# A conv-FFN whose down-projection trails the up-projection: half of its columns as seven block products

## The chip, the cores and the metric

One core of a Trainium2 chip runs the whole layer. The metric is device time of one execution in microseconds (us). TensorE (PE) multiplies, its weight loads are listed as PEld, VectorE is DVE, ScalarE is ACT, GpSimd is POOL, and SyncE (SP) issues the DMA transfers from HBM to the on-chip memory SBUF. Matmuls accumulate in PSUM, which has eight banks of 128 x 512 f32.

## The reference, cut to what matters

The layer is an attention mixer and then a conv-FFN, each added to `x` (256 tokens, 2048 columns). The change concerns the FFN:

```
def conv_ffn(h, w_up_l, conv_w_l, conv_b_l, w_down_l):
    u = h @ w_up_l                                  # 256 x 2048 @ 2048 x 11264
    u = causal depthwise convolution of width 3 over the tokens, + conv_b_l
    gate, val = jnp.split(u, 2, axis=-1)            # 5632 each
    return (jax.nn.silu(gate) * val) @ w_down_l     # 256 x 5632 @ 5632 x 2048
...
h = rms_norm(x, ffn_norm[layer])
x = x + conv_ffn(h, w_up[layer], conv_w[layer], conv_b[layer], w_down[layer])
```

All is f32. The kernel gets near f32 out of one-pass matmuls by splitting each operand into a rounded part `hi` (type fp32r) and the rest `lo`, and adding three products: hi x hi, hi x lo, lo x hi.

## The kernel before

**Weights.** `weights` (L202) makes one tile of weights ready: a DMA of up to 1 MB into `w_raw` (three buffers, L209), an ACT cast to `w_hi` (L210) and a DVE subtraction to `w_lo` (L211), two buffers each. The pool `wpool` is opened at the start and stays open to the end. The three instructions get a higher priority by `AHEAD`; a scheduler orders each engine's instructions by priority and by which buffers are free, and puts in the waits. Each engine then works strictly in that order.

**Attention.** Until about 413 us: the input projection, two kinds of attention as generators that advance one `step` per weight tile, and the output projection. That last one is `token_major` (L220) with `x` updated at L556; beside it `transposed_split` (L147) makes `hT`, the transposed and split activations of the FFN.

**FFN.** 44 tiles of 128 features for gate and 44 for value. `up_pair` (L603) makes two feature tiles: `feature_major` (L242) runs 16 blocks of k in two halves, one weight tile each; per k it does two matmuls of `w_hi` against hi and lo of `hT` together (512 columns, L250) and two of `w_lo` against hi alone (256 columns, L255). The accumulator has two banks. `summed` (L262) adds its halves out of PSUM (ACT copy L265, DVE L266), L588 scales by the token's norm, `convolved` (L582) does the convolution (ACT L592, four DVE steps L597), and L620 to L624 make SiLU, the product with the value and the split pair `g2`. Accumulators rotate over three places: two of pool `psa` and one of `psf`.

**Order of work.** `FFN_PARTS` cuts the 44 tiles into parts of 16, 16 and 12. For each part all up pairs come first, then the down-projection of the part, by `token_major` in four chunks of 512 columns: per weight tile of four k tiles 24 matmuls (L235, L236, L237: two token tiles, three products), and one addition to `x` (L630) at the end of a chunk. The last part's chunks are stored (L633). The parameters of the convolution (`crow`) are loaded early, at L118.

Of the kernel before, what the change touches and what calls it, by code (L numbers as in the profile page):

```python
# [8 lines left out]
F32 = mybir.dt.float32  # L9
F32R = mybir.dt.float32r  # L10
AF = mybir.ActivationFunctionType
ALU = mybir.AluOpType
AX = mybir.AxisListType

P = 128
D = 2048
S = 256
NT = S // P
# [6 lines left out]
NFT = DFF // P  # L25
# [11 lines left out]

AHEAD = 200
WINDOW = 2
FFN_PARTS = [(0, 16), (16, 32), (32, 44)]  # L40


@with_exitstack
def hybrid_layer(
# [19 lines left out]
    nc = tc.nc  # L64
    act, dve = nc.scalar, nc.vector
# [3 lines left out]
    of = out.rearrange("b s d -> (b s) d")  # L69
    wi, wo, wu, wd = w_in[0], w_out[0], w_up[0], w_down[0]  # L70

    const = ctx.enter_context(tc.tile_pool(name="const", bufs=1))
    wpool = ctx.enter_context(tc.tile_pool(name="wpool", bufs=3))
    big = ctx.enter_context(tc.tile_pool(name="big", bufs=1))
    small = ctx.enter_context(tc.tile_pool(name="small", bufs=4))
    psa = ctx.enter_context(tc.tile_pool(name="psa", bufs=2, space=bass.MemoryType.PSUM))
    psb = ctx.enter_context(tc.tile_pool(name="psb", bufs=2, space=bass.MemoryType.PSUM))

    def f32(t):
        return t.bitcast(F32)  # L80


    NC2 = 2 * NFT
    cs = const.tile([P, C_MF], F32, name="cs")
    prow = const.tile([50, P], F32, name="prow")
    crow = const.tile([NC2, 4, P], F32, name="crow")
    bf = const.tile([P, NH], F32, name="bf")
    x2 = big.tile([P, NT, D], F32, name="x2")
    xt = [x2[:, t, :] for t in range(NT)]
# [18 lines left out]
    def load_parameters(masks):  # L108
        r0 = KT
        for src, n in (  # L110
            (ffn_norm, KT), (out_norm_fox, NH), (out_norm_sb, NH), (q_norm, 1), (k_norm, 1)
        ):
            nc.sync.dma_start(prow[r0 : r0 + n, :], src[0].rearrange("(n p) -> n p", p=P))
            r0 += n
        nc.sync.dma_start(cs[:, P:], cst[:, P:C_MF])
        nc.sync.dma_start(masks, cst[:, C_MF:])
        nc.sync.dma_start(bf, b_forget.to_broadcast([P, NH]))
        nc.sync.dma_start(crow[:, :3, :], conv_w[0].rearrange("w (n p) -> n w p", p=P))  # L118
        nc.sync.dma_start(crow[:, 3, :], conv_b[0].rearrange("(n p) -> n p", p=P))

    def rsqrt(out_, ss, scale, n):
        a = small.tile([P, n], F32, name="rs_a", tag=f"rs_a{n}")
# [55 lines left out]
            dve.tensor_scalar(dg[t], ident, rstd[:, t : t + 1], None, op0=ALU.mult)  # L178
        return rstd, dg

    def in_every_partition(dg, n):
        R = const.tile([P, S], F32, name=f"R{n}")
        pr = psb.tile([P, S], F32, name="pr", tag="t")
        for t in range(NT):
            nc.tensor.matmul(pr[:, t * P : (t + 1) * P], ones, dg[t], start=t == 0, stop=t == NT - 1)
        dve.tensor_copy(R, pr)
        return R


    waiting = deque()  # L190

    def step():
        for g in list(waiting)[:WINDOW]:
            if next(g, g) is g:
                waiting.remove(g)
# [3 lines left out]
            step()  # L199


    def weights(src, a, b):  # L202
        raw = wpool.tile([P, 2048], F32, name="w_raw", tag="w_raw")
        hi = wpool.tile([P, 2048], F32R, name="w_hi", tag="w_hi", bufs=2)
        lo = wpool.tile([P, 2048], F32R, name="w_lo", tag="w_lo", bufs=2)
        n = a * b
        r3 = raw[:, :n].rearrange("p (a b) -> p a b", a=a)
        with tc.high_priority(offset=AHEAD):
            nc.sync.dma_start(r3, src)  # L209
            act.copy(hi[:, :n], raw[:, :n])  # L210
            dve.tensor_tensor(lo[:, :n], raw[:, :n], f32(hi[:, :n]), op=ALU.subtract)  # L211
        return (
            hi[:, :n].rearrange("p (a b) -> p a b", a=a),
            lo[:, :n].rearrange("p (a b) -> p a b", a=a),
        )

    def rows_of(w, k0, n, c0, cols):
        return w[k0 * P : (k0 + n) * P, c0 : c0 + cols].rearrange("(k p) c -> p k c", p=P)
# [23 lines left out]
    def feature_major(w, c0, pool, tag):  # L242

        acc = pool.tile([P, 2, 512], F32, name="pu", tag=tag)
        for kh in range(2):
            hi, lo = weights(rows_of(w, 8 * kh, 8, c0, 2 * P), 8, 2 * P)
            for i in range(8):
                k = 8 * kh + i
                for j in range(2):
                    nc.tensor.matmul(  # L250
                        acc[:, j, :], hi[:, i, j * P : (j + 1) * P],
                        hT[:, k].rearrange("p a b -> p (a b)"), start=k == 0, stop=False,
                    )
                for j in range(2):
                    nc.tensor.matmul(  # L255
                        acc[:, j, S:], lo[:, i, j * P : (j + 1) * P], hT[:, k, 0, :],
                        start=False, stop=k == KT - 1,
                    )
            step()
        return acc  # L260

    def summed(pool, acc, tag, **kw):  # L262

        t2 = pool.tile([P, 2, S], F32, name="t2", tag=tag, **kw)
        act.copy(t2, acc[:, :, S:])  # L265
        dve.tensor_tensor(t2, acc[:, :, :S], t2, op=ALU.add)  # L266
        return t2

    with ExitStack() as actx:
        at = actx.enter_context(tc.tile_pool(name="at", bufs=1))  # L270
        pss = actx.enter_context(tc.tile_pool(name="pss", bufs=2, space=bass.MemoryType.PSUM))
        tmp = actx.enter_context(tc.tile_pool(name="tmp", bufs=2))
# [77 lines left out]
        rstd1, dg1 = token_factors(ss1, 1)  # L350
# [19 lines left out]
        for j in range(3):  # L370
            acc = project(2 * WF + 344 * j, 344)
# [97 lines left out]


        B0 = 3 * WF + NH
        R1 = in_every_partition(dg1, 1)
        R1q = const.tile([P, S], F32, name="R1q")
        dve.tensor_scalar(R1q, R1, QSCALE, None, op0=ALU.mult)

        def sb_heads(c0, scale, name):
# [87 lines left out]
    ccol = const.tile([P, 4, NC2], F32, name="ccol")  # L564
    R = None

    def convolution_parameters():
        for i in range(4):
            pc = psb.tile([P, 512], F32, name="pcc", tag="t")
            nc.tensor.transpose(pc[:, :NC2], crow[:, i, :], ident[:NC2, :NC2])  # L570
            dve.tensor_copy(ccol[:, i, :], pc[:, :NC2])


    ff = ctx.enter_context(tc.tile_pool(name="ff", bufs=2))
    psf = ctx.enter_context(tc.tile_pool(name="psf", bufs=1, space=bass.MemoryType.PSUM))
    nu = 4
    up = [ff.tile([P, 2, 2 + S], F32, name=f"up{i}") for i in range(nu)]
    for u in up:
        dve.memset(u[:, :, 0:2], 0.0)
    n_up = 0  # L580

    def convolved(ps, f0):  # L582

        nonlocal n_up
        u = up[n_up % nu]
        n_up += 1
        t2 = summed(ff, ps, "t2")
        dve.tensor_tensor(u[:, :, 2:], t2, R.unsqueeze(1).to_broadcast([P, 2, S]), op=ALU.mult)  # L588
        a = ff.tile([P, 2, S], F32, name="cv", tag="cv", bufs=4)
        for j in range(2):  # L590
            f = f0 + j
            act.activation(  # L592
                a[:, j, :], u[:, j, 2:], AF.Identity,
                scale=ccol[:, 2, f : f + 1], bias=ccol[:, 3, f : f + 1],
            )
            for w in range(2):
                dve.scalar_tensor_tensor(  # L597
                    a[:, j, :], u[:, j, w : w + S], ccol[:, w, f : f + 1], a[:, j, :],
                    op0=ALU.mult, op1=ALU.add,
                )  # L600
        return a

    def up_pair(f0):  # L603

        nonlocal R, n_pair
        pool, tag = (psf, "pu") if n_pair % 3 == 2 else (psa, "acc")
        n_pair += 1
        acc = feature_major(wu, f0 * P, pool, tag)
        if R is None:
            R = in_every_partition(dg2, 2)  # L610
            convolution_parameters()
        return convolved(acc, f0)

    gT = {}
    n_pair = 0
    for n_part, (f_lo, f_hi) in enumerate(FFN_PARTS):
        for f in range(f_lo, f_hi, 2):
            gate = up_pair(f)
            val = up_pair(NFT + f)
            act.activation(gate, gate, AF.Silu)  # L620
            dve.tensor_tensor(gate, gate, val, op=ALU.mult)
            g2 = ff.tile([P, 2, 2, S], F32R, name="g2", tag="g2", bufs=12)
            act.copy(g2[:, 0], gate)  # L623
            dve.tensor_tensor(g2[:, 1], gate, f32(g2[:, 0]), op=ALU.subtract)  # L624
            for j in range(2):
                gT[f + j] = g2[:, :, j, :]
        for c in range(4):
            acc = token_major(lambda k: gT[f_lo + k], wd, f_lo, f_hi - f_lo, 512 * c, 512)
            xs = x2[:, :, c * 512 : (c + 1) * 512]
            dve.tensor_tensor(xs, acc, xs, op=ALU.add)  # L630
            if n_part == len(FFN_PARTS) - 1:
                for t in range(NT):
                    nc.sync.dma_start(of[t * P : (t + 1) * P, c * 512 : (c + 1) * 512], xs[:, t, :])  # L633


def _constants():
# [54 lines left out]
```

## Time and profile before

| | |
|---|---|
| device time, median of 3 | 1152.29 us (1151.68 to 1153.18) |
| the profiled execution | 1153.37 us |
| its span, first to last instruction | 1151.6 us |
| granted TensorE clock | 1.000 |
| moved by DMA | 211.39 MB, mean 184 GB/s |
| out-projection ends, FFN begins | 412.9 us |
| up pairs of the first part end | 593.3 us |
| second part: up, then down | 680.4 us, 858.7 us |

The page gives, per engine, busy time and its share of the span; then the chain of work that ended last, followed back from the last instruction; then groups of equal instructions by line, with how long the engine stood idle before them and what ended that. The timeline lists single instructions in order of time: start, duration, engine, line, operation, output and inputs. Idle time of an engine that is not on the chain costs nothing.

### The profile page before, as it was taken

To read this page: it belongs to the slowest core of one execution; us is meant where nothing else is said; L and a number is where in the kernel's file an instruction comes from. 1 tells how busy PE (TensorE), PEld (TensorE's weight loads), DVE (VectorE), ACT (ScalarE), POOL (GpSimd) and SP (SyncE) were. 2 spreads that over 40 slices of the span, in tenths; PEclk is the share of its full clock that TensorE was granted. 3 is DMA by queue.
4 is the path that set the end of the run, shared out by engine and by line. 5 is a ranking of instruction groups with operands and counts; after the bars stand their busy time and mean duration, and the time that the engine had idled before them with its cause. 6 is when DMAs were issued, how large, how long until landed. Compare 5 with 4: busy or idle time off the path is not lost.

```text
span 1151.6 us, 14371 instructions
## 1 busy us (share of the span) xinstructions
PE 1137.1 (99%) x6002; PEld 976.7 (85%) x6002; DVE 716.4 (62%) x798; ACT 551.9 (48%) x620; POOL 0.2 (0%) x4
## 2 busy tenths in 40 slices
PE   7999999999999999999999999999999999999998
PEld 5998888888888888888888888888888888888886
DVE  4646756646565667677774546767775455767753
ACT  4644454455564555555554334555554334555531
POOL 0000000000000000000000000000000000000000
PEclk9999999999999999999999999999999999999999
DMA  6766555564445545555556655555556655555562
GB/s 227 213 210 204 170 173 161 168 182 148 147 149 170 185 154 193 195 194 185 183 183 198 203 183 186 194 196 192 184 183 188 204 193 183 187 195 193 189 221 74
DMA packets 162540, 211.39 MB, mean 184 GB/s; under 512 B 3737, under 2 KB 117547, under 8 KB 162475
## 3 DMA queue, kind: packets, MB, share of 16 engines
q1 hardware_dynamic: 162474, 210.47, 56.7%
q8 instruction: 47, 0.77, 0.3%
q14 instruction: 19, 0.15, 0.0%
HBM read 208.36 MB, written 2.10 MB: 183 GB/s over the span
## 4 chain that ended last, share of the span: by engine, by line
PE 96%; DVE 1%; ACT 1%; DMA 1%; issue 1%; SPq 0%; ACTq 0%; DVEq 0%
PE pu L250 34%; PE pu L255 17%; PE acc L236 14%; PE acc L237 14%; PE acc L235 14%; ACT w_hi L210 1%; DVE w_lo L211 1%; PE ps_x L152 1%; DMA w_raw<-in_w_in_dram 0%; DMA masks<-in_cst_dram 0%; PE ps_z L492 0%; PE ps_h L284 0%; PE ps_s L425 0%; PE ps_o L452 0%; PE ps_o L518 0%
## 5 line engine op out<-in xcount | busy, mean ns | idle before, releaser
L211 DVE TENSOR_TENSOR w_lo<-w_raw,w_hi 128x2048 fp32r<-128x2048 f32 (+2 forms) x204 | 450.8, 2210 | 360.2 <-ACT w_hi L210 360.2
L210 ACT CAST w_hi<-w_raw 128x2048 fp32r<-128x2048 f32 (+2 forms) x204 | 375.9, 1843 | 512.4 <-issue 260.5
L250 PE MATMUL pu<-hT,w_hi 128*128 128x512 f32 x1664 | 523.5, 396 | 0.0
L255 PEld LDWEIGHTS pu<-hT,w_lo 128*128 128x128 f32 x1664 | 312.4, 188 | 73.9 <-DVE w_lo L211 0.4
L255 PE MATMUL pu<-hT,w_lo 128*128 128x256 f32 x1664 | 327.6, 278 | 0.0
L250 PEld LDWEIGHTS pu<-hT,w_hi 128*128 128x128 f32 x1664 | 253.8, 189 | 0.3
L236 PE MATMUL acc<-w_lo,g 128*128 128x512 f32 x352 | 137.1, 389 | 0.8 <-DVE w_lo L211 0.8
L235 PE MATMUL acc<-w_hi,g 128*128 128x512 f32 x352 | 137.1, 389 | 0.0
L237 PE MATMUL acc<-w_hi,g 128*128 128x512 f32 x352 | 136.9, 389 | 0.0
L235 PE MATMUL acc<-w_hi,hT 128*128 128x512 f32 (+1 forms) x320 | 120.2, 376 | 0.0
L236 PE MATMUL acc<-w_lo,hT 128*128 128x512 f32 (+1 forms) x320 | 119.2, 373 | 0.5 <-DVE w_lo L211 0.3
L237 PE MATMUL acc<-w_hi,hT 128*128 128x512 f32 (+1 forms) x320 | 119.0, 372 | 0.0
L236 PEld LDWEIGHTS acc<-w_lo,g 128*128 128x128 f32 x352 | 66.1, 188 | 14.8 <-DVE w_lo L211 1.3
L235 PEld LDWEIGHTS acc<-w_hi,g 128*128 128x128 f32 x352 | 66.1, 188 | 13.8 <-ACT g L623 0.3
L237 PEld LDWEIGHTS acc<-w_hi,g 128*128 128x128 f32 x352 | 66.1, 188 | 13.8
L597 DVE SCALAR_TENSOR_TENSOR cv<-up,ccol,cv 128x256 f32<-128x256 f32 x176 | 74.2, 480 | 2.2 <-ACT cv L592 2.0
L236 PEld LDWEIGHTS acc<-w_lo,hT 128*128 128x128 f32 x320 | 60.5, 189 | 9.6 <-DVE w_lo L211 1.5
L237 PEld LDWEIGHTS acc<-w_hi,hT 128*128 128x128 f32 x320 | 60.6, 189 | 8.8
L235 PEld LDWEIGHTS acc<-w_hi,hT 128*128 128x128 f32 x320 | 60.6, 189 | 8.1
L592 ACT ACTIVATE cv<-up,ccol 128x256 f32<-128x256 f32 x88 | 48.2, 591 | 8.0 <-DVE up L588 8.0
L235 PE MATMUL acc<-w_hi,oT 128*128 128x512 f32 x96 | 38.1, 397 | 0.0
L237 PE MATMUL acc<-w_hi,oT 128*128 128x512 f32 x96 | 37.5, 390 | 0.0
(146 smaller groups left out, 602.4 us busy)
## 6 DMA issues: line engine op xcount, KB each, us to landing
w_raw<-in_w_up_dram SPq DMA_DIRECT2D x88, 1024.0 KB, 5.1
w_raw<-in_w_down_dram SPq DMA_DIRECT2D x44, 1024.0 KB, 5.1
w_raw<-in_w_in_dram SPq DMA_DIRECT2D x36, 1024.0 KB, 5.3
w_raw<-in_w_out_dram SPq DMA_DIRECT2D x16, 1024.0 KB, 5.1
w_raw<-in_w_in_dram SPq DMA_DIRECT2D x12, 688.0 KB, 4.3
w_raw<-in_w_in_dram SPq DMA_DIRECT2D x8, 512.0 KB, 5.3
out_dram<-x SPq DMA_DIRECT2D x8, 256.0 KB, 3.6
x<-in_x_dram SPq DMA_DIRECT2D x3, 512.0 KB, 6.2
```

The lines of the kernel that those rows point to most:

```text
L152: nc.tensor.transpose(ps[:, j, t * P : (t + 1) * P], xt[t][:, (k + j) * P : (k + j + 1) * P], ident)
L210: act.copy(hi[:, :n], raw[:, :n])
L211: dve.tensor_tensor(lo[:, :n], raw[:, :n], f32(hi[:, :n]), op=ALU.subtract)
L235: nc.tensor.matmul(o, lhi, hi[:, i, :], start=first, stop=False)
L236: nc.tensor.matmul(o, lhi, lo[:, i, :], start=False, stop=False)
L237: nc.tensor.matmul(o, llo, hi[:, i, :], start=False, stop=last)
L250: nc.tensor.matmul(acc[:, j, :], hi[:, i, j * P : (j + 1) * P], hT[:, k].rearrange("p a b -> p (a b)"), start=k == 0, stop=False,)
L255: nc.tensor.matmul(acc[:, j, S:], lo[:, i, j * P : (j + 1) * P], hT[:, k, 0, :], start=False, stop=k == KT - 1,)
L592: act.activation(a[:, j, :], u[:, j, 2:], AF.Identity, scale=ccol[:, 2, f : f + 1], bias=ccol[:, 3, f : f + 1],)
L597: dve.scalar_tensor_tensor(a[:, j, :], u[:, j, w : w + S], ccol[:, w, f : f + 1], a[:, j, :], op0=ALU.mult, op1=ALU.add,)
```

## The change

The parts become five of eight tiles and one of four. A part's down-projection no longer follows it: it is put in a queue (`behind`), and `step`, which runs after each half of an up pair, takes steps from that queue while the next part's up-projection runs. `pace` spreads the 11 steps over the 16 half pairs of a part; in the last part, with 8 half pairs, it is doubled.

For columns 0 to 1023 the down-projection of a part is `down_in_seven`. The 256 tokens, the part's 8 k tiles and the 1024 columns are halved each, and the eight block products are replaced by seven products of sums of blocks (a Strassen scheme in Winograd's form). A product is 12 matmuls of 512 columns into one bank, and a bank is added to or taken from blocks of `x` while it still accumulates. The sums of activation blocks are made by `combinations`, on DVE, and split again; those of weight blocks by DVE additions into `w_sum` or a raw tile, then split. Columns 1024 to 2047 go by `down_plain`, as before but in single banks. The last part, of four tiles, is done plainly at the end.

To make room, `wpool` is closed with the attention and a new one is opened for the FFN, with four raw buffers and three of `w_hi` and `w_lo`; `crow` is loaded there, after the first weight tiles; the up-projection's accumulators rotate over the two places of `psa` alone; `up` has two buffers, `val` one.

```diff
-FFN_PARTS = [(0, 16), (16, 32), (32, 44)]
+FFN_PARTS = [(f, min(f + 8, NFT)) for f in range(0, NFT, 8)]
...
-    wpool = ctx.enter_context(tc.tile_pool(name="wpool", bufs=3))
...
     with ExitStack() as actx:
+        n_split = 2
+        wpool = actx.enter_context(tc.tile_pool(name="wpool", bufs=3))
...
+    n_split = 3
+    wpool = ctx.enter_context(tc.tile_pool(name="wff", bufs=4))
+    ff = ctx.enter_context(tc.tile_pool(name="ff", bufs=2))
+    psf = ctx.enter_context(tc.tile_pool(name="psf", bufs=2, space=bass.MemoryType.PSUM))
+    crow = ff.tile([NC2, 4, P], F32, name="crow", tag="val", bufs=1)
+    nc.sync.dma_start(crow[:, :3, :], conv_w[0].rearrange("w (n p) -> n w p", p=P))
+    nc.sync.dma_start(crow[:, 3, :], conv_b[0].rearrange("(n p) -> n p", p=P))
...
+    def split(raw, a, b):
+        hi = wpool.tile([P, 2048], F32R, name="w_hi", tag="w_hi", bufs=n_split)
+        lo = wpool.tile([P, 2048], F32R, name="w_lo", tag="w_lo", bufs=n_split)
+        n = a * b
+        act.copy(hi[:, :n], raw[:, :n])
+        dve.tensor_tensor(lo[:, :n], raw[:, :n], f32(hi[:, :n]), op=ALU.subtract)
...
+    def step():
+        nonlocal n_behind
...
+        n_behind += pace
+        while behind and n_behind >= 16:
+            if next(behind[0], behind) is behind:
+                behind.popleft()
+            else:
+                n_behind -= 16
...
+    def combinations(g1, g2):
+        a11, a21 = g1[:, :, :P], g1[:, :, P:]
+        a12, a22 = g2[:, :, :P], g2[:, :, P:]
+        s = ff.tile([P, 2, 4, 2, P], F32R, name="s", tag="s")
+        t = [ff.tile([P, 2, 2, P], F32, name="t2", tag="t2") for _ in range(2)]
+        t5, s2, s4, t7 = t[0][:, 0], t[0][:, 1], t[1][:, 0], t[1][:, 1]
+        dve.tensor_tensor(t5, a21, a22, op=ALU.subtract)
+        dve.tensor_tensor(s2, t5, a11, op=ALU.subtract)
+        dve.tensor_tensor(s4, a12, s2, op=ALU.add)
+        dve.tensor_tensor(t7, a11, a21, op=ALU.subtract)
+        for i in range(2):
+            act.copy(s[:, 0, 2 * i : 2 * i + 2], t[i])
+            dve.tensor_tensor(
+                s[:, 1, 2 * i : 2 * i + 2], t[i], f32(s[:, 0, 2 * i : 2 * i + 2]), op=ALU.subtract
+            )
...
+        bank_a = psf.tile([P, 512], F32, name="bank_a", tag="a")
+        with ahead():
+            w = wpool.tile([P, 2048], F32, name="w_sum", tag="w_sum", bufs=1)
+            load(w11, into=w)
+            parts = split(w, 4, 512)
+        product(bank_a, True, of_pairs(0, 0), parts)
+        add(x11, bank_a)
+        yield
+        bank_b = psb.tile([P, 512], F32, name="bank_b", tag="t")
+        with ahead():
+            dve.tensor_tensor(w, w, load(w12), op=ALU.add)
+            parts = split(w, 4, 512)
+        product(bank_b, True, of_sums(0), parts)
+        add(x22, bank_b)
+        yield
+        with ahead():
+            b22 = load(w22)
+            parts = split(b22, 4, 512)
+            dve.tensor_tensor(w, w, b22, op=ALU.add)
+        product(bank_b, False, of_sums(2), parts)
+        add(x12, bank_b)
+        yield
+        with ahead():
+            parts = split(w, 4, 512)
+        product(bank_a, False, of_sums(1), parts)
+        add(x12, bank_a, ALU.subtract)
+        yield
+        with ahead():
+            b12, b22 = load(w12), load(w22)
+            dve.tensor_tensor(b12, b12, b22, op=ALU.add)
+            parts = split(b12, 4, 512)
+        product(bank_a, False, of_sums(3), parts)
+        add(x22, bank_a, ALU.subtract)
+        yield
+        bank_c = psb.tile([P, 512], F32, name="bank_c", tag="t")
+        with ahead():
+            b21 = load(w21)
+            parts = split(b21, 4, 512)
+            dve.tensor_tensor(w, w, b21, op=ALU.add)
+        product(bank_c, True, of_pairs(1, 0), parts)
+        add(x11, bank_c)
+        yield
+        with ahead():
+            parts = split(w, 4, 512)
+        product(bank_a, False, of_pairs(1, 1), parts)
+        add(x21, bank_a)
+        yield
...
     for n_part, (f_lo, f_hi) in enumerate(FFN_PARTS):
...
+        pace = 11 * 8 // (f_hi - f_lo)
...
+            if len(pairs) > 2:
+                sums.append(combinations(gates[-3], gate))
+        while behind:
+            n_behind, pace = 16, 0
+            step()
+        if not last_part:
+            behind.append(down_in_seven(f_lo, pairs, sums, 0))
+            behind.append(down_plain(f_lo, pairs, 1024, 1024))
```

## Prediction

> **What bounds the kernel now.** I read the page first: busy shares, then the chain that ended last.
>
> ```profile
> span 1151.6 us, 14371 instructions
> PE 1137.1 (99%) x6002; PEld 976.7 (85%) x6002; DVE 716.4 (62%) x798; ACT 551.9 (48%) x620; POOL 0.2 (0%) x4
> PE 96%; DVE 1%; ACT 1%; DMA 1%; issue 1%; SPq 0%; ACTq 0%; DVEq 0%
> ```
>
> TensorE is 96% of the chain, so time is saved by taking matmuls away, as long as TensorE never waits. A busy matmul row is longer than the matmul's price, because matmuls overlap; the price is the distance between starts. So next came TensorE's timeline, where the second part's up-projection begins and ends:
>
> ```profile
> 593.29 0.40 PE L235 MATMUL acc<-w_hi,g 128*128 128x512 f32 x1
> ...
> 680.36 0.39 PE L250 MATMUL pu<-hT,w_hi 128*128 128x512 f32 x1
> ...
> 858.70 0.40 PE L235 MATMUL acc<-w_hi,g 128*128 128x512 f32 x1
> ```
>
> From 593.29 to 680.36 stand the 384 down matmuls of the first part: 87.07 / 384 = 0.227 us each. From 680.36 to 858.70 stand 16 up pairs: 178.34 / 16 = 11.15 us a pair, 5.57 a half pair (one weight tile of 1 MB). TensorE runs through without a gap. The busy table by stretches gives the other engines beside those 16 pairs (columns: stretch, its length, busy us of PE, PEld, DVE, ACT, POOL, granted clock, DMA share, GB/s):
>
> ```profile
> 680.00:859.00 179.00, 179.00 (x1029) 156.16 (x1028) 126.83 (x137) 90.88 (x92) 0.00 (x0) 1.00 0.58 189
> ```
>
> VectorE: 126.8 / 16 = 7.9 us of each 11.15.
>
> **What it removes.** In five parts of eight feature tiles, half of the columns are seven products of 12 matmuls, 84, where there were 96. That is 60 matmuls less: 60 x 0.227 = **-13.6 us**, all on the path. The built program's order agrees: 5870 TensorE instructions against 5930.
>
> **What it adds beside TensorE.** By the program's order: 15 more splits (an ACT cast of 1.91 us and a DVE subtraction each), 20 DVE additions of 128x2048, 10 more loads of 1 MB, the token combinations, and smaller additions to x. The 128x2048 f32 addition is not in this trace; its bounds are the ACT cast of that shape, 1.91 us, and four 128x512 additions (L621) of 0.69, 2.8 us. The nearest row is the DVE subtraction of the same shape and type of input, and I take that. A subtraction is followed by the next instruction after 2.21 us:
>
> ```profile
> 500.50 2.29 DVE L211 TENSOR_TENSOR w_lo<-w_raw,w_hi 128x2048 fp32r<-128x2048 f32 x1 [1.34 <-ACT w_hi L210]
> 502.71 1.66 DVE L597 SCALAR_TENSOR_TENSOR cv<-up,ccol,cv 128x256 f32<-128x256 f32 x4
> ```
>
> The dense stretch of a part is its first 11 half pairs with the seven products between: TensorE 11 x 5.57 + 84 x 0.227 = 80.3 us. DVE there: 11/16 of 8 x 7.9 = 43.6; seven splits and four additions at 2.21, 24.3; seven additions of a bank at 0.70 (the 128x512 rows take 0.68 to 0.75), 4.9; half of the combinations, 2.9; sum 75.7, 94%. It fits, narrowly, so order decides. I walked one middle part through the DVE's order. A split can start once TensorE has left the tile three before it (three buffers); cast and subtraction take 4.2 us, and the rest is DVE's queue. The tightest place is the product on w12+w22. TensorE leaves a half pair; 4.3 us later the fourth product's split is done; then stand a bank addition 0.70, the sum 2.21 and the next half pair's split 2.21: 9.4 us. TensorE has 2.72 + 5.57 + 2.72 = 11.0 us to do meanwhile. Slack 1.6 us, elsewhere 2 to 6. So in the four middle parts I cost all this at **0**; without that slack each us more costs 4. The two loads that this sum needs land in time by the 5.1 us row below (the second with about 1 us to spare), on SP's queue ahead of nothing that is due sooner.
>
> **Into the FFN.** The weight pool is now closed with the attention and a new one opened. In the program's order the first up load waits for the *last* matmul of the output projection, and three loads follow it at once; the small conv loads come after them and are needed 10 us later. In the trace of before, the first w_up load was issued at 393.8 and its use began at 412.92, with no gap:
>
> ```profile
> 412.69 0.39 PE L237 MATMUL acc<-w_hi,hT 128*128 128x512 f32 x1
> 412.92 0.39 PE L250 MATMUL pu<-hT,w_hi 128*128 128x512 f32 x1
> ```
>
> The bare chain: matmul ends 413.1, issue 0.1, landing, cast 1.91, subtraction 2.29, signals 0.2. Landing by the rows of 1 MB loads:
>
> ```profile
> DMA to landing us min/median/max: 5.0/5.1/6.1
> ```
>
> I take 5.3, as three more follow closely (bounds 5.0 and 6.9, the longest in the run). First w_lo: 422.9. TensorE meanwhile does two hi matmuls (0.5) and the eight transposes and two small matmuls (1.3) that it has to do anyway: 422.9 - 412.9 - 1.8 = **+8.2 us** (7.9 to 9.8). Then the rate after the gap. The only place in the trace where TensorE comes out of idleness is the start:
>
> ```profile
> 11.23 0.63 PE L235 MATMUL acc<-w_hi,hT 128*128 128x512 f32 x1
> 11.66 0.63 PE L236 MATMUL acc<-w_lo,hT 128*128 128x512 f32 x1
> ...
> 15.94 0.39 PE L236 MATMUL acc<-w_lo,hT 128*128 128x512 f32 x1
> 16.17 0.39 PE L237 MATMUL acc<-w_hi,hT 128*128 128x512 f32 x1
> ```
>
> 0.43 us apart until 13.8, 0.23 later: ten matmuls cost 2.0 us too much, while the granted-clock column says 1.00. I take **+2.0** (0 to 2.1) after this gap. The Trainium skill, "TensorE: Matmul & The Clock Gate", Part 1, says that the array's clock halves after an idle window of about 3.4 us and comes back after as long of sustained work. The trace's start agrees with half rate; an estimate by that page would put 1.7 in place of 2.0, and its gate also speaks for the charge after a gap of this length.
>
> **The last part** has four tiles, so the pace doubles: the first two half pairs are each followed by a product, the third by two. The DVE's order there: TensorE leaves the first half pair at 5.6 (from its start); the second product's split is done at 9.8; then come a bank addition 0.7, a sum 2.2, a split 2.2, three conv steps 1.2, a split 2.2, conv 0.4, gate times value 0.7, two differences 0.8, the sum w12+w22 2.2, a g2 subtraction 0.7, and the fourth product's split 2.2: 25.4. TensorE is there at 2.72 + 5.57 + 1.36 + 5.57 after 5.6, plus one hi matmul: 21.1. Wait 4.3, and then about 1 for the next half pair's cast, whose buffer came free late: **+5.5** (3 to 8, since one such queue was summed by hand). At the very end the last value's chain is covered by two plain steps, 10.9 us, and half a chunk: +0.5.
>
> **Sum**: -13.6 + 8.2 + 2.0 + 5.5 + 0.5 = +2.6 on the profiled execution, 1153.37 (span 1151.6 and 1.8 around it), so 1156.0. The median shown is 1.08 below that execution; against it 1152.29 + 2.6 = **1154.9, say 1155 us**.
>
> **Rivals.**
> - *The whole saving* (the first load does not in fact wait, and no split is late): 1152.3 - 13.6 = 1138.7. Only the order's wait speaks against it, but plainly. 0.04.
> - *Faster, the splits come in time*: the last part's queue is shorter than my sum, or TensorE keeps its rate. Without both it is -13.6 + 8.2 + 0.5 = -4.9: 1147.4; the turn comes where all stalls together are under 13.6. For it: the stalls are sums over one engine's queue with mean durations, and one landing more or less moves them. Against it: the waits themselves stand in the order. 0.20.
> - *VectorE becomes the bound* in the dense stretches: the 1.6 us of slack is spent on DVE waiting for ACT between its conv steps (ACT casts of 1.91 stand in the same queue). At 3 us beyond it, four parts cost 12: 1155 + 12 = 1167. For it: 94% leaves 4.6 us per stretch for every such wait. Against: the plain stretch that follows has 5 x 5.57 + 96 x 0.227 = 49.6 us of TensorE for about 34 of DVE, and all other splits have 2 us or more to spare. 0.22.
> - The forecast, 1150 to 1159: 0.54.
>
> A measurement of this kernel can tell about 0.2% (2.3 us) from no change. Faster by more: 0.04 + 0.17 of the second rival = 0.21. Within: 0.20 of the forecast and 0.03 of the second rival = 0.23. Slower: 0.34 + 0.22 = 0.56. The range runs from 1146 to 1166; it leaves out the whole saving and the ends of the two others.
>
> **What would show it.** Down matmuls 0.227 apart and 60 fewer; a TensorE gap of about 8 us between the output projection's last matmul and the first lo matmul of the up-projection, then starts 0.43 apart for some 4 us; one wait of about 4 us in the last part on w_lo; none over 1 us in the middle parts, where w_lo precedes its product by 1.6 us or more; DVE near 75% of the span. Wrong if the gap is missing, or if TensorE waits on w_lo in every part.

## The result and the profile after

The changed kernel takes 1167.87 us (median; 1167.31 to 1169.31), the kernel before, beside it, 1152.41: ratio 1.0136 (1.0118 to 1.0153), 15.5 us slower. The prediction of 1155.0 was 12.9 too low, and its range ended at 1166. From here on "the part with index 1" is the second of the six: the first one with products between its half pairs.

The page of the changed kernel, lines as shown for the kernel before:

```profile
span 1165.8 us, 14514 instructions
PE 1139.1 (98%) x5942; PEld 970.6 (83%) x5942; DVE 841.2 (72%) x938; ACT 590.7 (51%) x655; POOL 0.2 (0%) x4
PE 94%; DVE 2%; ACT 1%; DMA 1%; issue 1%; SPq 0%; ACTq 0%; DVEq 0%
PEclk9999999999999989998999999999999999998999
```

60 matmuls are gone and yet PE is busy 2 us longer; VectorE has 2% of the chain where it had 1%; and the clock row, all 9 before, has three notches. Each notch follows a stall. TensorE's timeline at the entry to the FFN, in the part with index 1, and in the last part:

```profile
411.18 0.39 PE L239 MATMUL acc<-w_hi,hT 128*128 128x512 f32 x1
...
416.97 1.19 PE L181 MATMUL pr<-dg,cs 128*128 128x128 f32 x4 [3.02 <-DVE dg L174]
...
420.88 0.80 PE L257 MATMUL pu<-hT,w_lo 128*128 128x256 f32 x2 [1.13 <-DVE w_lo L209]
...
541.09 0.63 PE L675 MATMUL bank_b<-w_hi,s 128*128 128x512 f32 x1 [2.32 <-ACT s L650]
543.50 1.22 PE L675 MATMUL bank_b<-w_hi,s 128*128 128x512 f32 x2 [1.35 <-DVE s L651]
...
1066.62 0.53 PE L675 MATMUL bank_a<-w_hi,s 128*128 128x512 f32 x1 [1.81 <-ACT w_hi L208]
1068.98 0.79 PE L675 MATMUL bank_a<-w_lo,s 128*128 128x512 f32 x1 [1.83 <-DVE w_lo L209]
...
1076.21 0.73 PE L252 MATMUL pu<-hT,w_hi 128*128 128x512 f32 x2 [0.83 <-ACT w_hi L208]
```

The brackets give idle time and releaser. The first and the third stall were forecast. The second was not: the product on the token combinations waits for the last pair's s. The table by stretches, cut where the granted clock changes (columns as in the prediction: the granted clock is the third figure from the end), shows what a stall leaves behind: the clock is at half for a while.

```profile
415.00:425.30 10.30, 6.83 (x21) 5.27 (x22) 6.75 (x12) 5.72 (x5) 0.00 (x0) 0.50 1.10 351
541.30:548.10 6.80, 5.45 (x15) 3.98 (x15) 5.88 (x8) 3.89 (x6) 0.00 (x0) 0.50 0.48 154
1067.00:1073.80 6.80, 4.97 (x12) 3.80 (x12) 6.27 (x6) 1.72 (x3) 0.00 (x0) 0.50 0.48 154
663.00:791.00 128.00, 128.00 (x678) 108.92 (x677) 107.15 (x104) 67.03 (x62) 0.00 (x0) 1.00 0.62 204
```

The last row lies in the middle parts: no stall, VectorE busy 107.15 of 128. But even there a down matmul costs more than before. One plain step of 24, from its first matmul to the next half pair:

```profile
605.26 0.40 PE L747 MATMUL bank_a<-w_hi,g 128*128 128x512 f32 x1
...
610.86 0.62 PE L252 MATMUL pu<-hT,w_hi 128*128 128x512 f32 x2
```

5.60 / 24 = 0.233 us each, 0.227 before. All 996 FFN down matmuls have it, those at the very end too, whose code is the old one; the attention's and the output projection's still have 0.227.

So there are four suspects: the closed pool, the late combinations, the doubled pace of the last part, and something that slows each down matmul. Medians of all runs, with the kernel before at 1152.4 to 1152.8 beside them:

| kernel | us | against |
|---|---|---|
| changed, pool kept open | 1160.92 | -7.0, changed |
| changed, combinations earlier | 1158.99 | -8.9, changed |
| changed, pace 11 in the last part | 1162.37 | -5.5, changed |
| changed, 64 bytes of padding | 1168.05 | +0.2, changed |
| changed, 192 bytes of padding | 1162.59 | -5.3, changed |
| before, weights elsewhere | 1152.46 | 0.0, before |
| before, the same and a new pool for the FFN | 1162.46 | +10.0, the row above |
| before, 64 bytes ahead of g | 1159.93 | +7.5, before |
| before, 64 bytes ahead of everything | 1152.50 | -0.3, before |
| four edits, 64 bytes | 1146.41 | -21.5, changed |
| four edits, 192 bytes | 1140.19 | -27.7, changed |
| the same, all products plain | 1152.37 | +12.2, the row above |

### The profile page after: what moved, and what is told of

Read it like the earlier page. It is cut to its first block, busy times and chain, and to the rows that moved or that the text cites. A ratio compares the mean times of both kernels' runs of the same rounds, so it can differ in the third digit from the quotient of the medians.

```text
span 1165.8 us, 14514 instructions
## 1 busy us (share of the span) xinstructions
PE 1139.1 (98%) x5942; PEld 970.6 (83%) x5942; DVE 841.2 (72%) x938; ACT 590.7 (51%) x655; POOL 0.2 (0%) x4
## 4 chain that ended last, share of the span: by engine, by line
PE 94%; DVE 2%; ACT 1%; DMA 1%; issue 1%; SPq 0%; ACTq 0%; DVEq 0%
PE pu L252 33%; PE pu L257 16%; PE acc L237 8%; PE acc L238 8%; PE acc L239 8%; PE bank_a L675 5%; PE bank_a L749 3%; PE bank_a L747 3%; PE bank_a L748 3%; PE bank_b L675 2%; DVE w_lo L209 1%; PE bank_c L675 1%; ACT w_hi L208 1%; PE ps_x L148 1%; DMA x<-in_x_dram 0%
## 5 line engine op out<-in xcount | busy, mean ns | idle before, releaser
L209 DVE TENSOR_TENSOR w_lo<-w_raw,w_hi 128x2048 fp32r<-128x2048 f32 (+2 forms) x199 | 438.9, 2206 | 233.2 <-ACT w_hi L208 232.4
L208 ACT CAST w_hi<-w_raw 128x2048 fp32r<-128x2048 f32 (+2 forms) x199 | 366.0, 1840 | 376.2 <-issue 139.8
L252 PEld LDWEIGHTS pu<-hT,w_hi 128*128 128x128 f32 x1664 | 259.2, 190 | 6.8 <-ACT w_hi L208 1.9
L747 PE MATMUL bank_a<-w_hi,g 128*128 128x512 f32 x160 | 63.2, 395 | 0.0
L749 PE MATMUL bank_a<-w_hi,g 128*128 128x512 f32 x160 | 63.1, 395 | 0.0
L748 PE MATMUL bank_a<-w_lo,g 128*128 128x512 f32 x160 | 63.1, 394 | 0.0
L209 DVE TENSOR_TENSOR w_lo<-w_sum,w_hi 128x2048 fp32r<-128x2048 f32 x20 | 45.8, 2291 | 14.6 <-ACT w_hi L208 14.6
L208 ACT CAST w_hi<-w_sum 128x2048 fp32r<-128x2048 f32 x20 | 38.1, 1904 | 23.4 <-PE pu L252 23.4
L606 DVE SCALAR_TENSOR_TENSOR val<-up,ccol,val 128x256 f32<-128x256 f32 x88 | 39.7, 481 | 3.8 <-ACT val L601 3.4
L606 DVE SCALAR_TENSOR_TENSOR gate<-up,ccol,gate 128x256 f32<-128x256 f32 x88 | 37.9, 481 | 0.9 <-ACT gate L601 0.7
L238 PE MATMUL acc<-w_lo,oT 128*128 128x512 f32 x96 | 37.4, 389 | 0.0
```

The costliest lines, as they stand in the source:

```text
L238: nc.tensor.matmul(o, lhi, lo[:, i, :], start=False, stop=False)
L252: nc.tensor.matmul(acc[:, j, :], hi[:, i, j * P : (j + 1) * P], hT[:, k].rearrange("p a b -> p (a b)"), start=k == 0, stop=False,)
L606: dve.scalar_tensor_tensor(a[:, j, :], u[:, j, w : w + S], ccol[:, w, f : f + 1], a[:, j, :], op0=ALU.mult, op1=ALU.add,)
L747: nc.tensor.matmul(acc[t], g[:, 0, ts], hi[:, i, :], start=first, stop=False)
L748: nc.tensor.matmul(acc[t], g[:, 0, ts], lo[:, i, :], start=False, stop=False)
L749: nc.tensor.matmul(acc[t], g[:, 1, ts], hi[:, i, :], start=False, stop=last)
```

## The experiments

**The closed pool, taken back.** The old pool stays open; a new one gives only the tiles that the FFN needs beyond the attention's.

```diff
-    wpool = ctx.enter_context(tc.tile_pool(name="wff", bufs=4))
+    extra, n_raw, n_hi = ctx.enter_context(tc.tile_pool(name="wff", bufs=1)), 0, 0
...
+        pool, bufs = (extra, 1) if extra and n_hi % 3 == 0 else (wpool, 2)
```

> The changed kernel, but the old weight pool (three raw tiles, two splits) stays open through the FFN, and a small extra pool gives the fourth raw tile, the third split and the sum tile. Theory 'the closed pool makes the entry gap': the first w_up load no longer waits for the last output projection matmul, the gap of about 7.7 us goes and with it the 2.2 us that the half granted clock behind it cost: 1167.9 - 9.9 = 1158. Rival 'the gap only moves': the third split comes from the pool that still waits for the attention, and the gap comes two half pairs later: 1166 to 1168. Side question, the spacing of the FFN's down matmuls (0.233 us in the changed kernel, 0.227 before): two of three weight tiles now lie where the attention's lay, which had 0.227 there. If the address of the moving tile sets it, two thirds of 996 matmuls win 0.006 each, 4 us more (1154); if not, the spacing stays 0.233 for all.

1160.92 (1157.27 to 1164.78), where 1158 was expected. The gap is gone: the trace goes from the output projection to the up-projection in one step.

```profile
412.39 0.39 PE L250 MATMUL acc<-w_hi,hT 128*128 128x512 f32 x1
412.62 0.61 PE L263 MATMUL pu<-hT,w_hi 128*128 128x512 f32 x2
```

The spacing stays 0.233 for all three weight tiles, so their address is not its cause. The wide spread is a finding too: mean granted clock and time of the five runs go together (0.998 and 1157.27, 0.996 and 1158.07, 0.993 and 1160.92, 0.992 and 1162.42 and 1164.78). The stalls of the two later places are still there, and what they cost in clock differs from run to run: in the profiled one, of 1158.07 us, each is followed by 3.41 us at half clock, where the table above has 6.8.

**The closed pool, put into the kernel before**, and as its base the kernel before with the weight tiles at other addresses:

```diff
-    wpool = ctx.enter_context(tc.tile_pool(name="wpool", bufs=3))
...
     small = ctx.enter_context(tc.tile_pool(name="small", bufs=4))
+    wpool = ctx.enter_context(tc.tile_pool(name="wpool", bufs=3))
```

> The kernel before, with one line moved: the weight pool is opened behind the pools of x and of the small tiles, so the weight tiles lie at 77408 to 134752 bytes of each partition, near where the changed kernel has them, in place of 25696 to 83040. Theory 'address of the weights': its 1056 FFN down matmuls go from 0.227 to 0.233 us, +6.7: 1159. Rival 'the spacing has another cause' (the place of the stationary g tiles, or the work beside): 0.227 stays, 1152.4, no difference.

1152.46: no difference, spacing 0.227. Then in place of that line a pool within the attention, and one of the same size ahead of ff:

```diff
+        wpool = actx.enter_context(tc.tile_pool(name="wpool", bufs=3))
...
+    wpool = ctx.enter_context(tc.tile_pool(name="wff", bufs=3))
     ff = ctx.enter_context(tc.tile_pool(name="ff", bufs=2))
```

> The kernel before, with that one part of the change alone: the weight pool (at the same addresses as in the run just above) closes with the attention and an equal one opens for the FFN. Theory 'closed pool': a gap of 7 to 8 us between the output projection and the first lo matmul, and about 2.2 us more at half the granted clock behind it: +10 against the run just above (1162 without a change of spacing, 1169 with it). Rival: the scheduler fetches ahead nevertheless, +0 to +2.

1162.46, +10.0. The timeline has the same gap, here with nothing else of the change around it:

```profile
412.50 0.39 PE L236 MATMUL acc<-w_hi,hT 128*128 128x512 f32 x1
...
423.11 0.80 PE L254 MATMUL pu<-hT,w_lo 128*128 128x256 f32 x2 [0.74 <-DVE w_lo L210]
```

**The combinations, earlier.**

```diff
-        dve.tensor_tensor(t5, a21, a22, op=ALU.subtract)
...
+        with tc.high_priority(offset=AHEAD):
+            dve.tensor_tensor(t5, a21, a22, op=ALU.subtract)
...
```

> The changed kernel with one edit: the token combinations get the same priority as the weight splits. In the changed kernel the first part with products waits 2.6 and 2.0 us for the last pair's combinations, and the granted clock is halved for 6.8 us behind that (about 3.4 us lost). Theory 'the combinations stand too far back in the queues': both go, 1167.9 - 4.6 - 3.4 = 1160. Rival 'VectorE is full there': the wait moves to a split of the same stretch, and the time stays within 2 us, 1166 to 1168.

1158.99. Why the combinations were late is in the order of two queues of the changed kernel. On VectorE a sum and a split of weights, 4.4 us, stand ahead of the product of gate and value, from which the combinations are made:

```profile
532.02 2.29 DVE L706 TENSOR_TENSOR w_sum<-w_sum,w_raw 128x2048 f32<-128x2048 f32 x1
534.23 2.28 DVE L209 TENSOR_TENSOR w_lo<-w_raw,w_hi 128x2048 fp32r<-128x2048 f32 x1
536.43 0.69 DVE L766 TENSOR_TENSOR gate<-gate,val 128x512 f32<-128x512 f32 x1
```

On ScalarE the cast of the next weight tile then stands ahead of the casts to s, and waits for TensorE itself:

```profile
537.15 0.62 ACT L768 CAST g<-gate 128x512 fp32r<-128x512 f32 x1 [3.59 <-DVE gate L766]
538.62 1.90 ACT L208 CAST w_hi<-w_raw 128x2048 fp32r<-128x2048 f32 x1 [0.85 <-PE pu L252]
540.43 1.13 ACT L650 CAST s<-t 128x512 fp32r<-128x512 f32 x2
```

With the edit the product of gate and value starts at 525.47, the last cast to s at 530.46, and the product on s starts without a wait:

```profile
530.46 0.63 ACT L651 CAST s<-t 128x512 fp32r<-128x512 f32 x1 [0.32 <-DVE t L648]
...
533.57 0.40 PE L676 MATMUL bank_b<-w_hi,s 128*128 128x512 f32 x1
```

The same work in another order leaves no wait in this part, so VectorE was not full there; the rival falls. It is 1 us more than expected: the last part gained as well, with three stalls (1.5, 0.8 and 1.4 us from one start to the next, in place of 2.1, 2.4 and 1.2) and no halved clock behind them in that trace.

**The pace of the last part.**

```diff
-        pace = 11 * 8 // (f_hi - f_lo)
+        pace = 11
```

> The changed kernel with the pace of the eight-tile parts (11 of 16) in the last part too, where it was 22: five products lie between its eight half pairs, two products and the four plain steps behind them. Theory 'the doubled pace makes VectorE's queue late': the three waits of the last part (2.1, 2.4 and 1.2 us) and the 6.8 us of halved clock behind them go: 1167.9 - 5.7 - 3.4 = 1158.8. Rival 'the wait moves': with two products close together at the end their splits come late, 3 us or more remain: 1162 to 1167.

1162.37, just within the rival's 1162 to 1167, and yet the three stalls and the notch in the clock are gone. One new stall stands later, 1.0 us, where two plain steps of different columns meet and the second waits for the addition to x (L753):

```profile
1120.35 0.47 PE L747 MATMUL bank_a<-w_hi,g 128*128 128x512 f32 x1 [1.01 <-DVE x L753]
```

The gain of 9.1 us that was expected was too high. The three stalls hold 4.5 us of idle time, and the halved stretch 4.97 us of PE's work, which costs half of that: 7.0 us as an estimate, less the new 1.0; 5.5 were measured.

**The place of g and s.** With the weights' address out, the places of the other operand were left. In the built program of the kernel before, g begins at byte 163680 of each partition; in the changed one, with fewer `up` tiles ahead of it, at 179872. Padding tells:

```diff
     up = [ff.tile([P, 2, 2 + S], F32, name=f"up{i}", bufs=1) for i in range(2)]
+    pad = ff.tile([P, 16], F32, name="pad", bufs=1)
+    dve.memset(pad, 0.0)
```

> The changed kernel with 64 bytes of padding in each partition ahead of the g and s tiles, and nothing else. In the kernel before the g tiles begin at 163680 bytes, 96 above a multiple of 128, as all weight tiles, hT and oT do in both kernels; in the changed kernel, which has fewer up tiles ahead of them, g and s begin 32 above a multiple of 128 (179872). Theory 'place of the stationary tile': the down matmuls go back from 0.233 to 0.227 us apart, 996 x 0.0065 = 6.5: 1167.9 - 6.5 = 1161.4. Rival 'work beside TensorE' (SBUF traffic of the splits, sums and loads): the spacing stays 0.233, 1166 to 1169.

> The kernel before with the same 64 bytes ahead of its g tiles, which brings them to 32 above a multiple of 128. Theory 'place of the stationary tile': its 1056 FFN down matmuls go from 0.227 to 0.233 us, +6.9: 1159.3. Rival 'work beside TensorE': no difference, 1152.4.

The two disagree: the changed kernel stays at 1168.05, but the kernel before goes to 1159.93. Its first 384 down matmuls take 682.71 - 593.12 = 89.59, 0.2333 each, where they took 87.07:

```profile
593.12 0.39 PE L235 MATMUL acc<-w_hi,g 128*128 128x512 f32 x1
...
682.71 0.62 PE L250 MATMUL pu<-hT,w_hi 128*128 128x512 f32 x2
```

So the place counts, and 128 bytes is the wrong unit. Modulo 256 the weight tiles begin at 96 in all of these; g at 96 in the kernel before (fast), at 160 in the changed one and in the padded kernel before (slow), at 224 in the padded changed one (slow). That gives two questions: does 96 cure the changed kernel (48 in place of 16 in the edit above), and is it 96 or the distance to the moving tile (16 columns ahead of everything)?

> The changed kernel with 192 bytes of padding ahead of the g and s tiles. In the slow cases so far g began 160 or 224 above a multiple of 256 bytes, in the fast one (the kernel before) 96, as the weight tiles in all of them. Now g and s are at 96 too. Theory 'place of g and s, modulo 256': 0.227 us again, 996 x 0.0063 = 6.3 less: 1161.6. Rival 'what makes the changed kernel slow there is not the place, and only the kernel before reacts to it': 1168.

> The kernel before with 64 bytes of padding ahead of everything, so that the stationary and the moving tiles move together, from 96 to 160 above a multiple of 256. If the place of the stationary tile relative to the moving one counts: 0.227 us everywhere, 1152.4. If the place itself counts: the FFN's down matmuls go to 0.233 (+6.9) and those of the attention and the output projection, 576 of 512 columns and 288 of 344, with them (+5): 1159 to 1165.

1162.59 and 1152.50: it is the distance between the two tiles. The plain step of the changed kernel with 192 bytes takes 5.45 / 24 = 0.227:

```profile
607.20 0.40 PE L749 MATMUL bank_a<-w_hi,g 128*128 128x512 f32 x1
...
612.65 0.61 PE L252 MATMUL pu<-hT,w_hi 128*128 128x512 f32 x2
```

**All edits together**, first with 64 bytes, then with 192:

> All four edits at once: the pool kept open, the combinations with the splits' priority, the pace of 11 in the last part, the 64 bytes. If the four causes are separate and complete, only the 60 saved matmuls are left of the change: 1152.4 - 13.6 = 1138.8, plus at most 3 us of small waits (1138 to 1142). Rival: a further cost that the four hide, such as a busy VectorE in the parts that were never disturbed: 1145 or more.

> The kernel with all four edits, with 192 bytes in place of 64. That kernel took 1146.4 with its down matmuls 0.233 us apart. Theory 'place of g and s': 996 x 0.0063 = 6.3 less, 1140.1, and with that the 60 matmuls are the whole difference from the kernel before. Rival: the spacing stays, 1146.

1146.41 (0.9955, 0.9941 to 0.9969), over what was expected by the 6.2 of the spacing, which 64 bytes do not cure. With 192: **1140.19, ratio 0.9896 (0.9882 to 0.9909), faster than both kernels.** Its page (span 1137.7 us):

```profile
PE 1123.1 (99%) x5942; PEld 965.0 (85%) x5942; DVE 836.9 (74%) x939; ACT 590.9 (52%) x655; POOL 0.2 (0%) x4
PE 96%; DVE 1%; DMA 1%; ACT 1%; issue 0%; SPq 0%; ACTq 0%; DVEq 0%
```

VectorE is as busy as in the changed kernel, and its share of the chain is back at 1%.

**The products themselves.**

```diff
-            behind.append(down_in_seven(f_lo, pairs, sums, 0))
-            behind.append(down_plain(f_lo, pairs, 1024, 1024))
+            behind.append(down_plain(f_lo, pairs, 0, 2048))
```

> The kernel just above with plain products for all columns: eight steps of 24 matmuls a part in place of seven of 12 and four of 24, and without the token combinations; the order and the pools stay. Theory 'beside the four causes the seven products are worth their matmuls': 60 x 0.227 = 13.6 more than the kernel just above, 1153 to 1154. Rival 'the seven products' VectorE work costs something in the dense stretches': a difference of under 10.

1152.37, +12.2 against the kernel with seven products, where 13.6 was expected and the rival had under 10, and equal to the kernel before. So spreading the steps costs and brings nothing by itself; the seven products bring the change's whole gain.

## Why the prediction was wrong

Its steps, in its own order:

- **Matmuls taken away, -13.6.** Right: 12.2 between the last two kernels. The one with seven products has a stall of 1.6 us from start to start, the plain one of 0.8, which is half of the 1.4 us missing.
- **The dense stretches, 0.** This is the step that failed. The words were "I walked one middle part through the DVE's order" and "in the four middle parts I cost all this at 0". For three of the four that was right: PE is busy 128.00 of 128.00. The first of them, the part with index 1, has another order, and the walk does not hold there. VectorE begins gate times value of the last pair 24 us after that pair's last matmul (512.1 to 536.43), with seven sums and splits of weights between; in the next part it is 15 us (644.4 to 659.81), with four. Then the casts' order on ScalarE adds its share. The cost was 3.7 us of idle time and the halved clock behind it, 8.9 us with what followed in the last part. In the later parts a plain step of 5.6 us, left over from the part before, stands in TensorE's order between the last pair and the first product; nothing is left over from part 0. That this missing step makes the difference fits the order, but no run shows it by itself.
- **The price of a matmul.** 0.227 us was taken for matmuls whose operands the change had moved. 996 x 0.0063 = 6.3 us (5.3 and 6.2 by the runs with 192 bytes) stood in no term and no rival. The diff shows the moved pools, but no row of the trace of before shows that their place matters.
- **Into the FFN, +8.2 and +2.0.** Right: 420.88 - 411.18 - 0.23 - 1.8 = 7.7 us, and +10.0 by the new pool alone in the kernel before. Taking it back in the changed kernel gave only 7.0, within the wide spread of that run.
- **The last part, +5.5.** Place, cause and size of the stalls were right (4.5 us idle); the rate behind them was left out, though the step into the FFN had charged just that. Its cure was worth 5.5, with a new stall of 1 us in it.
- **The rivals.** The nearest by time, VectorE as the bound at 1167, came close by luck: VectorE is no less busy at 1140.19 us. It did name a queue in which ScalarE's casts stand in the way; one part had that, not four. Of the signs listed, the gap, the last part's wait and three of the four middle parts came as told; the spacing of 0.227 did not, nor did "none over 1 us in the middle parts".

The sum closes: the four edits are worth 27.7 us where the terms for cost stood at 8.2 + 2.0 + 5.5 + 0.5 = 16.2, and the products saved 12.2 where 13.6 stood; the differences, 11.5 and 1.4, are the 12.9 us missed (the 0.5 for the very end has no edit of its own). One by one the edits gave 7.0 + 8.9 + 5.5 + 5.3 = 26.7; the rest is smaller than the spread of the run with the pool kept open.

## What to carry to other kernels

Walk the first and the last turn of a pipelined loop, not only a middle one: there the queues are in another order, and one that never shows elsewhere can set the time. A stall of a few microseconds can be charged once more, with the clock behind it, at each place. After moving pools, compare the distance between the starts of equal matmuls with the one before, and look at the byte offsets of both operands if it has changed.

## What the runs showed of the hardware

- **Two tiles' distance sets the price of a matmul.** fp32r, 512 columns: 0.2267 us (87.07 / 384) where the stationary and the moving tile begin at the same place modulo 256 bytes, 0.2333 (89.59 / 384) where they are 64 apart, and about the same on average at 128 (0.233 in the changed kernel with 64 bytes of padding). Other distances were not tried. The Trainium skill, "TensorE: Matmul & The Clock Gate", Part 2, "Step-by-step: what each phase is for", says that loading the next tile's weights doesn't take SBUF read bandwidth from the running matmul, as the two have ports of their own. Here the place of one tile against the other costs 3%, which ports of their own do not explain, and the measurement decides. What the two share stays open.
- **The clock after a stall.** The halved stretches last 3.41 us (the run with the pool kept open), 6.83 or 10.24 us (the changed kernel), in steps of one length. The same page, Part 1, "What's actually happening", has a window of 3413 ns that runs freely, and the trace agrees: the three halved stretches of the changed kernel begin 126.3 and 525.7 us apart, 37.0 and 154.0 of that length. It also has the clock drop after an idle window of that length. Here less was enough: the 3.41 us that end at 541.3 hold 2.32 us of idle time, those that end at 1067.0 hold 1.81. The stalls of the run with the combinations earlier (1.5, 0.8 and 1.4 us from start to start) cost no clock. Where the line runs between the two was not measured; the kernel with the pool kept open, with idle stretches of 1.7 to 2.3 us at two places, took 1157.27 to 1164.78 us.
